# A hybrid decoder layer: the Strassen sums of the second MLP weights made by accumulating DMAs, some signs moved to the other operand, and later squares in FF1

## The chip, the cores and the metric

The kernel runs on one core of one Trainium2 chip. The metric is the device time of one execution in microseconds (us), as the median of several runs. A separate profiled execution gives the trace from which all other times below are read.

## The reference

One decoder layer on x of 1024 x 1024 (tokens x channels, float32), with a conditioning vector c. Cut to what matters:

```python
mod = silu(c) @ w_ada + b_ada
sh1, sc1, gt1, sh2, sc2, gt2 = split(mod, 6)
u = x * (1 + sc1) + sh1
proj = u @ w_in                       # queries, keys, values, DeltaNet inputs, gates
y_a = sliding_window_attention(qa, ka, va, sinks) @ w_oa      # 16 heads, window 128
y_b = gated_deltanet(dq, dk, dv, z, b_raw, a_raw) @ w_ob      # 8 heads of 128, chunks of 64
mixed = (sigmoid(g_a) * y_a + sigmoid(g_b) * y_b) @ w_out
x = layer_norm(ALPHA * x + (1 + gt1) * mixed)
u2 = x * (1 + sc2) + sh2
h = square(relu(u2 @ w_ff1 + b_ff1))                          # 1024 -> 4096: FF1
x = layer_norm(ALPHA * x + (1 + gt2) * (h @ w_ff2 + b_ff2))   # 4096 -> 1024: FF2
```

## The kernel before

Every large float32 product is made of three matmuls: each operand is split in a high part, which ACT rounds to the fast 32-bit type (L215), and a low part, which DVE subtracts (L216); PE adds high x high, high x low and low x high in PSUM. A matmul is 128 x 128 by 128 x 512 nearly everywhere.

The stages, with their place in the profiled execution:

- The adaLN head (to about 60 us): loads of w_ada and x by SP, the modulation rows, and u in its split form.
- The keys stage (about 60 to 260 us; L525 to L697): values and DeltaNet keys of eight heads. A head's projection on PE runs through `fm_unit` (L186 to L188), then come transposes (L664), the decay (L616), a mask on POOL (L627) and key products (L688), with their results stored in DRAM.
- The gate, query and key units and the attention (about 240 to 570 us). `stream_unit` (L236, its matmul is L248) runs 48 matmuls of a 128-channel unit of the projection. In between stand 64 attention slots (L929): the scores on PE (L834 and L835), the maximum and the exponential on DVE and ACT (L842, L849), the joining of the two key blocks' weights on POOL (L853, `join`), the scaling on ACT (L861), a transpose on PE (L877, `att_turn`), its split (L883, L887), a mask on POOL (L894), the product with the values on PE (L909), and for every second slot a store by POOL (L925).
- The head stage (about 580 to 940 us): DeltaNet for eight heads, with the query and value units.
- The two output projections, then the mixing (L1493) with the first layer norm and u2.
- FF1 (about 1240 to 1560 us) and FF2 (to the end), each as one level of the Strassen-Winograd scheme: seven products in place of eight, with sums of blocks formed ahead. FF1 makes 16 block rows x 7 products x 12 matmuls (L1866), FF2 the matmuls of L1926. DVE adds up FF1's blocks (`add_`, L1544), ACT applies relu and square (`square`, L1592; its operations are L1594 and L1595), and `h_sums` (L1613) and `h_sums2` (L1623) form sums of the result for FF2, which go to DRAM (hf_d).

The sums of w_ff2's blocks, which FF2 reads from DRAM (wt_d), are made by POOL. For each of 16 pairs of 128 rows `t_load` (L1681) loads 512 KB twice into SBUF, `t_make` (L1691) makes four differences of 128 x 512 (`sub`, L1436) and stores 512 KB twice in wt_d. Thirteen pairs lie in FF1, three at the start of FF2.

What sets the order: from L702 on, PE, DVE and ACT run in the order in which the code issues their instructions (`tc.manual_schedule(engines=order_all)`). The code keeps a counter of matmuls (`count`) and a heap of events: `at(p, f)` issues f when the counter reaches p, and `after(n, f)` n matmuls later (L197 to L207). SP and POOL are not in that list, and neither is anything ahead of L702: there the tile scheduler orders the instructions itself, by their dependencies and priorities, and an `at` sets for a DMA on SP or POOL no more than where the code issues it. `Q0` (L704) is the counter's value at which the head stage's own plan starts, 48 x the number of units ahead of it; `E0`, `F0` and `G0` are the starts of the mixing, FF1 and FF2.

SP issues nearly all loads, among them those of the projection weights (`load_raw`, L130, tiles wr of 512 KB); an engine's instructions and DMA issues run in order, and one that waits holds up those behind it.

Of the kernel before, what the change touches and what calls it, by code (L numbers as in the profile page):

```python
# [9 lines left out]
F32 = mybir.dt.float32  # L10
# [3 lines left out]
ALU = mybir.AluOpType  # L14
# [3 lines left out]
P = 128  # L18
D = 1024
# [15 lines left out]
def hybrid_layer_kernel(ctx: ExitStack, tc: tile.TileContext,  # L35
                        x, c, w_ada, b_ada, w_in, conv_w, a_log, dt_bias, sinks, dn_norm_w,
                        w_oa, w_ob, w_out, ln1_g, ln1_b, w_ff1, b_ff1, w_ff2, b_ff2,
                        ln2_g, ln2_b, out, dbg=None):
    nc = tc.nc
    x, c, out = x[0], c[0], out[0]  # L40
# [40 lines left out]
    wt_d = dram.tile([D_FF // (2 * P), 2, P, D], F32, name="wt_d")  # L81
# [60 lines left out]
    NPAIR, EARLY = NF // 2, 5  # L142
# [49 lines left out]
    halves = [slice(0, HALF), slice(HALF, 2 * HALF)]  # L192


    events, count, order = [], [0], [0]

    def at(p, f, *args):  # L197
        order[0] += 1
        heapq.heappush(events, (p, order[0], f, args))

    def after(n, f, *args):
        at(count[0] + n, f, *args)
# [275 lines left out]
    for step in ('t0 s0 o00 o01 w0 w1 d4 t1 s1 v203 o10 v235 o11 v256 m0 t2 p2 s2 v304 o20 v346 o21 m1 t3 p3 s3 v404 o30 v446 o31 m2 '  # L478
                 't4 p4 s4 v504 o40 v546 o41 m3 t5 p5 s5 r0 v604 o50 v646 o51 m4 t6 p6 s6 v704 o60 v746 o61 m5 t7 p7 s7 o70 o71 m6').split():
        f, k = step[0], int(step[1])  # L480
# [44 lines left out]
    with tc.tile_pool(name="pa", bufs=2, side="right") as pa:  # L525
        if True:
            ba = pv.tile([P, NT, 16], F32, name="ba")
            for t in range(NT):
                tok = slice(t * P, (t + 1) * P)
                pt = psum("ab"[t % 2], 2) if t < 4 else mm_tile()  # L530
# [12 lines left out]
                if t:  # L543
                    vd = pa.tile([P, 4, 64], F32, tag="vd", name="vd", bufs=1)
                    a, b = (vraw, pv4) if t % 2 == 0 else (pv4, vraw)
# [26 lines left out]
            for m in (13, 11, 9, 7, 5, 3, 1):  # L572
# [5 lines left out]
                                   op0=ALU.mult, op1=ALU.mult)  # L578
# [448 lines left out]
    def ada_part(f, b):  # L1027
# [23 lines left out]
                V.tensor_tensor(out=sc2, in0=g1c, in1=sc2, op=ALU.mult)  # L1051
        after(4, put)

    items = [(f, k) for f in range(KT) for k in range(KT + (f < 4))]
    at(Q0 + 20, ada_open)
    for i, (f, k) in enumerate(items):
# [324 lines left out]
    def mix_done(second, q, t, pt):  # L1381
        r = rs[t]
        rq = r[:, halves[q]]
        tm = pe.tile([P, HALF], F32, tag="t", name="tm", bufs=6)
        V.tensor_tensor(out=tm, in0=pt, in1=gt1[:, halves[q]], op=ALU.mult)
        V.scalar_tensor_tensor(out=rq, in0=rq, scalar=ALPHA, in1=tm, op0=ALU.mult, op1=ALU.add)
        V.bn_stats(out=parts[:, t, q, :], in_=rq)
        if not second:
            return
        st = pe.tile([P, 4], F32, tag="st", name="st", bufs=3)  # L1390
        V.bn_aggr(out=st[:, 0:2], in_=parts[:, t].rearrange("p q s -> p (q s)"))
        lag = {6: 20, 7: 12}.get(t, 1)
        after(lag, lambda: A.activation(out=st[:, 2:3], in_=st[:, 1:2], func=AF.Sqrt, bias=eps_ln))

        def norm():
            V.reciprocal(out=st[:, 3:4], in_=st[:, 2:3])
            V.tensor_scalar(out=r, in0=r, scalar1=st[:, 0:1], scalar2=st[:, 3:4], op0=ALU.subtract, op1=ALU.mult)
            nc.gpsimd.dma_start(out=res_d[t], in_=r)
        after(lag + 3, norm)
# [35 lines left out]
    def sub(E, out, a, b):  # L1435
        E.tensor_tensor(out=out, in0=a, in1=b, op=ALU.subtract)  # L1436
# [49 lines left out]


    w_more()
    for p in [1, 13] + [SEG * s + o for s in (0, 2) for o in (61, 73, 86, 98)] + [3 * SEG + o for o in (79, 85, 106, 114, 128)]:
        at(E0 + p, w_go)  # L1490
        at(E0 + p + 8, w_more)

# [11 lines left out]
    for s in range(4):  # L1504
        q, t0 = (0, 1, 1, 0)[s], 4 * (s // 2)
        if s != 2:
            del wt[:]
        groups = [[0, 1], [2, 3]] if s < 2 else [[4, 5], [6, 7]] if s == 2 else [[4, 5], [6], [7]]
        for ts in groups:
            pts = []  # L1510
            for t in ts:
                tag = ("mm", "a", "mm", "c", "mm", "a")[bank % 6]
                bank += 1
                pts.append(psum(tag, {"mm": 3, "a": 2, "c": 1}[tag]))
            for c in range(4):
                if len(wt) == c:
                    run_events(count[0])
                    wt.append(ready.pop(0))
                for pt, t in zip(pts, ts):
                    mix_mm(pt, slice(t * P, (t + 1) * P), c)  # L1520
            for pt, t in zip(pts, ts):
                at(max(count[0] + (14 if s == 2 and t > 5 else 1), E0 + 28), mix_done, s % 2 == 1, q, t, pt)
                if s % 2 == 1:
                    at(count[0] + 1, u2_done, t, count[0] + {6: 46, 7: 40}.get(t, 34))

# [17 lines left out]
    def add_(E, out, a, b):  # L1543
        E.tensor_tensor(out=out, in0=a, in1=b, op=ALU.add)  # L1544
# [53 lines left out]
    def full(i, c, pt):  # L1598
        t = tls[i, c]
        add_(V, t, t, pt)  # L1600
        after(3, square, i, c)

    def last_block(i, c, pt):
        t = tile_of(i, c)
# [4 lines left out]
    def again(i):  # L1609

        nc.sync.dma_start(out=tile_of(i, 0), in_=hf_d[0, i])

    def h_sums(i):  # L1613

        a11, a21, a22 = tls[i, 0], tls[i, 1], tls[i, 3]
        sa = sums_[i] = big2.tile([P, 2, HALF], F32, tag="h7", name="sa")
        sub(V, sa[:, 1], a11, a21)
        add_(V, a21, a21, a22)
        sub(V, sa[:, 0], a21, a11)
        put(5, i, a21)  # L1620
        nc.sync.dma_start(out=hf_d[5:7, i].rearrange("m p c -> p m c"), in_=sa)

    def h_sums2(i):  # L1623

        sb = big2.tile([P, 2, HALF], F32, tag="l7", name="sb")[:, 0]
        sub(V, sb, tls[i, 2], sums_[i][:, 0])
        put(3, i, sb)


# [40 lines left out]
    for i in range(NPAIR):  # L1670
        e = max(pos[i, 3], pos[i, 7]) + 12
        if i < EARLY:
            at(e - 24, again, i)
        at(e + 12, h_sums, i)
        at(pos[i, 4] + 20, h_sums2, i)

    wpair = {}

    def t_load(n):  # L1681
        if n < T_IN:
            ts = [big2.tile([P, D], F32, tag=f"{c}6", name="wx") for c in "hl"]
        else:
            ts = [wp.tile([P, D], F32, tag="wr", name="wx", bufs=2) for c in "hl"]
        wpair[n] = ts
        for j in range(2):
            f = n + NPAIR * j
            nc.gpsimd.dma_start(out=ts[j], in_=w_ff2[f * P:(f + 1) * P, :])

    def t_make(n):  # L1691
        (b11, b12), (b21, b22) = [[t[:, h] for h in halves] for t in wpair[n]]
        sub(G, b11, b12, b11)
        sub(G, b12, b22, b12)
        sub(G, b22, b22, b11)
        sub(G, b21, b21, b22)
        for j in range(2):
            nc.gpsimd.dma_start(out=wt_d[n, j], in_=wpair[n][j])

    T_IN, T_STEP = 13, 72  # L1700
    for n in range(NPAIR):
        p = pos[EARLY, 1] - 60 + T_STEP * n if n < T_IN else G0 + 60 + T_STEP * (n - T_IN)
        at(p, t_load, n)
        at(p + 24, t_make, n)

# [52 lines left out]
    def rows_sums():  # L1758
        G2, B2 = rows_["G2"], rows_["B2"]
        V.tensor_scalar(out=G2, in0=G2, scalar1=ALPHA, scalar2=None, op0=ALU.mult)  # L1760
        V.tensor_tensor(out=B2, in0=B2, in1=rows_["gt2"], op=ALU.mult)
        V.scalar_tensor_tensor(out=B2, in0=rows_["lb"], scalar=ALPHA, in1=B2, op0=ALU.mult, op1=ALU.add)

    def rr_load(t):
        rr[t] = big.tile([P, D], F32, tag=f"{'hl'[t // 4]}{4 + t % 4}", name="rr")
# [239 lines left out]
```

## Time and profile before

| | |
|---|---|
| median of 3 runs | 1883.41 us (1881.8 to 1889.56) |
| the profiled execution | 1882.44 us |
| its span, first to last instruction | 1880.3 us |
| mean granted TensorE clock | 0.989 of full speed |
| PE busy | 1827.3 us, 97% of the span |
| DVE, ACT, POOL busy | 1309.7, 978.0 and 411.7 us |

Busy time of PE includes matmuls that overlap in its pipeline, so a stretch in which PE is busy all the time may still run at less than its best rate; the granted clock and the number of matmuls of a stretch show that. In a group of instructions the numbers behind the bar are the busy time in us, the mean of one in ns, and the idle time of the engine just before, with what ended it. In a row of a DMA the numbers are KB of one transfer and us from its issue to its landing. Releasers are inferred from semaphore events.

### The profile page before, as it was taken

The numbers are of one execution on the slowest core, as the hardware profiler recorded it, in microseconds if no ns is written. First come the engines' busy times: TensorE is split into PE (matmuls) and PEld (weight loads), VectorE is DVE, ScalarE is ACT, GpSimd is POOL, SyncE is SP. The second block draws the span as 40 slices with busy tenths as digits, with TensorE's granted clock in tenths as the row PEclk, the third lists the DMA queues.
The fourth block names the chain that finished last, engine by engine and source line by source line (L and its number), as shares of the span: only waits on it lengthen the run. The fifth ranks groups of instructions, "written<-read, shape, count | busy, mean of one in ns | idle before, by whom it ended". The sixth has DMA issues, their size and how long they took to land.

```text
span 1880.3 us, 26014 instructions
## 1 busy us (share of the span) xinstructions
PE 1827.3 (97%) x9161; PEld 1509.4 (80%) x9161; DVE 1309.7 (70%) x2409; ACT 978.0 (52%) x2105; POOL 411.7 (22%) x509
## 2 busy tenths in 40 slices
PE   7999999999999999999999999999899999999997
PEld 5977788788888888888878888877687888888886
DVE  7677598998865666666554445788877566676697
ACT  3789666666654454554553322475454555434441
POOL 7323223433331000000001100014545102300000
PEclk7999999999999999999999999999999999999999
DMA  9655632232258454554346543359887549965571
GB/s 258 183 185 194 218 96 82 75 95 70 71 188 224 144 152 129 147 148 133 111 165 213 182 146 135 134 176 312 294 277 267 185 131 405 388 199 169 195 263 45
DMA packets 261644, 337.72 MB, mean 180 GB/s; under 512 B 25237, under 2 KB 170342, under 8 KB 261258
## 3 DMA queue, kind: packets, MB, share of 16 engines
q1 hardware_dynamic: 224042, 215.04, 36.4%
q0 software_dynamic: 30560, 108.44, 16.9%
q10 hardware_dynamic: 6912, 12.59, 1.8%
q8 instruction: 72, 1.18, 0.3%
q14 instruction: 58, 0.48, 0.1%
HBM read 231.40 MB, written 102.51 MB: 178 GB/s over the span
## 4 chain that ended last, share of the span: by engine, by line
PE 75%; DVE 11%; ACT 5%; issue 3%; DMA 2%; POOL 0%; ACTq 0%; SPq 0%; DVEq 0%; POOLq 0%
PE mm L248 33%; PE mm L1926 6%; PE mm L1866 6%; PE b L1926 4%; PE a L1926 4%; PE b L1866 3%; PE mm L1499 2%; DVE wl L216 2%; PE c L1926 2%; PE c L909 2%; PE a L1499 1%; PE a L1866 1%; PE mm L188 1%; PE mm L187 1%; PE mm L186 1%
## 5 line engine op out<-in xcount | busy, mean ns | idle before, releaser
L248 PE MATMUL mm<-uh,wl 128*128 128x512 f32 x800 | 331.3, 414 | 0.0
L248 PE MATMUL mm<-ul,wh 128*128 128x512 f32 x800 | 320.7, 401 | 0.0
L248 PE MATMUL mm<-uh,wh 128*128 128x512 f32 x800 | 317.4, 397 | 0.0
L216 DVE TENSOR_TENSOR sp<-sraw,sp 128x1024 fp32r<-128x1024 f32 x112 | 140.3, 1288 | 70.8 <-ACT sp L215 70.8
L215 ACT ACTIVATE sp<-sraw 128x1024 fp32r<-128x1024 f32 x112 | 112.7, 1054 | 121.6 <-PE b L1926 73.8
L248 PEld LDWEIGHTS mm<-ul,wh 128*128 128x128 f32 x800 | 150.6, 188 | 26.6 <-issue 0.2
L248 PEld LDWEIGHTS mm<-uh,wl 128*128 128x128 f32 x800 | 151.2, 189 | 22.9 <-issue 3.9
L248 PEld LDWEIGHTS mm<-uh,wh 128*128 128x128 f32 x800 | 151.2, 189 | 21.2 <-issue 0.2
L1926 PE MATMUL mm<-sp 128*128 128x512 f32 x528 | 136.5, 390 | 0.5 <-DVE sp L216 0.5
L1436 POOL TENSOR_TENSOR wx<-wx 128x512 f32<-128x512 f32 x64 | 100.3, 1567 | 77.4 <-DMA wx<-in_w_ff_dram 75.7
L1926 PEld LDWEIGHTS mm<-sp 128*128 128x128 f32 x528 | 98.6, 188 | 21.0 <-DVE sp L216 0.9
L216 DVE TENSOR_TENSOR wl<-wr,wh 128x1024 fp32r<-128x1024 f32 x81 | 98.6, 1218 | 8.1 <-ACT wh L215 7.9
L215 ACT ACTIVATE wh<-wr 128x1024 fp32r<-128x1024 f32 x81 | 85.0, 1049 | 22.2 <-PE c L1499 14.0
L216 DVE TENSOR_TENSOR wl<-fraw,wh 128x1024 fp32r<-128x1024 f32 x43 | 61.3, 1426 | 46.1 <-ACT wh L215 46.1
L1926 PE MATMUL a<-sp 128*128 128x512 f32 x336 | 92.5, 389 | 0.0
L1594 ACT ACTIVATE t<-t 128x512 f32<-128x512 f32 x48 | 30.1, 626 | 98.0 <-DVE t L1544 98.0
L1926 PE MATMUL b<-sp 128*128 128x512 f32 (+1 forms) x336 | 80.0, 374 | 0.0
L1169 ACT ACTIVATE vn<-a,brk 128x128 f32<-128x128 f32 x64 | 23.5, 367 | 108.2 <-PE a L1167 107.3
L842 DVE CUSTOM_DVE_ANT_0 nscore<-a,amask,nsink 128x256 f32<-128x256 f32 (+1 forms) x128 | 54.6, 464 | 33.4 <-PE a L835 32.7
L853 POOL TENSOR_TENSOR sm<-sm 128x256 f32<-128x256 f32 x56 | 55.6, 993 | 97.7 <-ACT sm L849 65.0
L1926 PEld LDWEIGHTS a<-sp 128*128 128x128 f32 x336 | 63.1, 188 | 13.1
L1926 PEld LDWEIGHTS b<-sp 128*128 128x128 f32 x336 | 60.5, 188 | 11.2
(520 smaller groups left out, 4718.3 us busy)
## 6 DMA issues: line engine op xcount, KB each, us to landing
wr<-in_w_in_dram SPq DMA_DIRECT2D x60, 512.0 KB, 3.6
sraw<-hf_d SPq DMA_DIRECT2D x56, 512.0 KB, 4.3
fraw<-in_w_ff_dram SPq DMA_DIRECT2D x32, 512.0 KB, 5.1
wx<-in_w_ff_dram POOLq DMA_DIRECT2D x32, 512.0 KB, 6.1
wt_d<-wx POOLq DMA_DIRECT2D x32, 512.0 KB, 4.2
sraw<-wt_d SPq DMA_DIRECT2D x32, 512.0 KB, 4.8
hf_d<-t ACTq DMA_DIRECT2D x48, 256.0 KB, 3.3
sraw<-in_w_ff_dram SPq DMA_DIRECT2D x24, 512.0 KB, 7.0
```

The costliest lines, as they stand in the source:

```text
L215: A.activation(out=hi, in_=src, func=AF.Copy)
L216: after(lag, lambda: V.tensor_tensor(out=lo, in0=src, in1=hi.bitcast(F32), op=ALU.subtract))
L248: T.matmul(ts[half], lhsT=w[:, k, :], rhs=xx[k][:, sl], start=k == 0 and m == 0, stop=k == KT - 1 and m == 2)
L842: V.tensor_tensor_reduce(out=ns[:, i, 1:1 + W], in0=sc[:, i * 2 * P:i * 2 * P + W], in1=amask[:, mo:mo + W], scale=-1.0, scalar=nsink[:, 2 ...
L853: G.tensor_tensor(out=sm[:, :, 1 + P:1 + 2 * P], in0=sm[:, :, 1:1 + P], in1=sm[:, :, 1 + P:1 + 2 * P], op=ALU.add)
L909: T.matmul(av[:, 0:256], lhsT=vt[:, b, :], rhs=p_[:, m, :], start=p_ is full and m == 0, stop=p_ is prods[-1][1] and m == 1)
L1169: after(1, lambda: A.activation(out=vn, in_=Wp[:, 0:P], func=AF.Copy, scale=brk[:, n, h:h + 1]))
L1436: E.tensor_tensor(out=out, in0=a, in1=b, op=ALU.subtract)
L1499: T.matmul(pt, lhsT=m[k][:, tok], rhs=w[:, k % 2, :], start=k == 0 and w is wh and m is mh, stop=k == KT - 1 and m is ml)
L1594: A.activation(out=t, in_=t, func=AF.Relu)
L1866: T.matmul(pt, lhsT=a[:, k0 + k, :], rhs=b[k], start=begin and k == 0 and x_ == 0, stop=k == 3 and x_ == 2, skip_group_check=True)
L1926: T.matmul(to, lhsT=a[:, f, t * P:(t + 1) * P], rhs=b[:, f, lo:up], start=(begin or own) and s % NS == 0 and f == 0 and x_ == 0, stop=s % ...
```

## The change

- The 32 loads, 64 differences and 32 stores of `t_load` and `t_make` go. In their place, in eight batches of two pairs, SP copies two blocks of 1 MB of w_ff2 into wt_d, DRAM to DRAM (`t_copy`), and POOL issues four accumulating DMAs of 512 KB (`t_acc`), which add DRAM rows to DRAM rows: the first two add a half of w_ff2 to a copied half, the third adds the first's result to the other block, and the fourth adds the third's result. They are given counter positions in the head stage (from Q0 + 40 on).
- With additions alone some sums come out with the opposite sign. `h_sums` and `h_sums2` form the other operand with opposite signs (`minus`), and the second half of the row gt2 is negated once (in `rows_sums`).
- `square` of a full FF1 block is issued 14 matmuls after its sum in place of 3, `h_sums` and `h_sums2` 12 matmuls later.
- In the mixing some lags (norm of tile 6, `mix_done` of tile 7, `u2_done`) and four points of its weight splits (`w_go`) move.

```diff
+    def w2_rows(b, n, h):
+        return w_ff2[(b * NPAIR + n) * P:(b * NPAIR + n + TB) * P, h].rearrange("(n p) c -> n p c", p=P)
+
+    def t_copy(n):
+        for b in range(2):
+            nc.sync.dma_start(out=wt_d[n:n + TB, b], in_=w2_rows(b, n, slice(0, D)))
+
+    def t_acc(n, i):
+        one, two = wt_d[n:n + TB, 0], wt_d[n:n + TB, 1]
+        dst, src = [(one[:, :, halves[0]], w2_rows(0, n, halves[1])), (one[:, :, halves[1]], w2_rows(1, n, halves[1])),
+                    (two[:, :, halves[1]], one[:, :, halves[0]]), (two[:, :, halves[0]], two[:, :, halves[1]])][i]
+        nc.gpsimd.dma_start(out=dst, in_=src, accum_op=ALU.add)
+
+    TB = 2
+    for n in range(0, NPAIR, TB):
+        p = Q0 + 40 + 60 * n
+        at(p, t_copy, n)
+        for i in range(4):
+            at(p + (30, 34, 64, 94)[i], t_acc, n, i)
...
-        lag = {6: 20, 7: 12}.get(t, 1)
+        lag = {6: 26, 7: 12}.get(t, 1)
...
-    for p in [1, 13] + [SEG * s + o for s in (0, 2) for o in (61, 73, 86, 98)] + [3 * SEG + o for o in (79, 85, 106, 114, 128)]:
+    for p in [1, 13] + [SEG * s + o for s in (0, 2) for o in (61, 73, 86, 98)] + [3 * SEG + o for o in (79, 100, 112, 118, 130)]:
...
-                at(max(count[0] + (14 if s == 2 and t > 5 else 1), E0 + 28), mix_done, s % 2 == 1, q, t, pt)
+                lag = 14 if s == 2 and t > 5 else 10 if s == 3 and t == 7 else 1
+                at(max(count[0] + lag, E0 + 28), mix_done, s % 2 == 1, q, t, pt)
                 if s % 2 == 1:
-                    at(count[0] + 1, u2_done, t, count[0] + {6: 46, 7: 40}.get(t, 34))
+                    at(count[0] + 1, u2_done, t, count[0] + {4: 30, 5: 36, 6: 48, 7: 42}.get(t, 34) - lag + 1)
...
-        after(3, square, i, c)
+        after(14, square, i, c)
...
+    def minus(out, a, b):
+        V.scalar_tensor_tensor(out=out, in0=a, scalar=-1.0, in1=b, op0=ALU.mult, op1=ALU.subtract)
+
...
-        add_(V, a21, a21, a22)
-        sub(V, sa[:, 0], a21, a11)
+        sub(V, a21, a22, a21)
+        minus(sa[:, 0], a21, a11)
...
-        sub(V, sb, tls[i, 2], sums_[i][:, 0])
+        minus(sb, tls[i, 2], sums_[i][:, 0])
...
-        at(e + 12, h_sums, i)
-        at(pos[i, 4] + 20, h_sums2, i)
-    def t_load(n):
...
-    def t_make(n):
...
+        at(e + 24, h_sums, i)
+        at(pos[i, 4] + 32, h_sums2, i)
...
+        gt = rows_["gt2"][:, halves[1]]
+        V.tensor_scalar(out=gt, in0=gt, scalar1=-1.0, scalar2=None, op0=ALU.mult)
```

More of the change, by code (lines that the diff above doesn't have):

```diff
@@ L1673, in hybrid_layer_kernel @@
             at(e - 24, again, i)
-        at(e + 12, h_sums, i)
-        at(pos[i, 4] + 20, h_sums2, i)
-    wpair = {}
-    def t_load(n):
[L1682 to L1689, printed above, removed]
-    def t_make(n):
[L1692 to L1704, printed above, removed]
+        at(e + 24, h_sums, i)
+        at(pos[i, 4] + 32, h_sums2, i)
     ORDER = (1, 2, 6, 5, 3, 7, 4)
```

## The prediction, made before the changed kernel ran

> **What bounds it now.** I read the page first, then the windows, the waits of PE, the groups of DVE, and the DMA and queue views of the stages that the change enters.
>
> ```profile
> PE 1827.3 (97%) x9161; PEld 1509.4 (80%) x9161; DVE 1309.7 (70%) x2409; ACT 978.0 (52%) x2105; POOL 411.7 (22%) x509
> ```
>
> PE is busy for 97% of the 1880.3 us span (the profiled run took 1882.44 us, the median is 1883.41, so the sum below starts from 1882.4 and needs no correction over 1 us). What can be gained is the little that PE loses; what can be lost is anything that makes PE wait. The windows show both, as busy time of PE, PEld, DVE, ACT and POOL, then PE's granted clock, DMA share and GB/s.
>
> ```profile
> 100.00:140.00 40.00, 39.78 (x211) 30.94 (x210) 33.47 (x93) 35.82 (x89) 12.37 (x20) 1.00 0.53 176
> 140.00:180.00 40.00, 40.00 (x195) 31.17 (x194) 29.65 (x71) 38.49 (x88) 14.88 (x22) 1.00 0.63 213
> ...
> 1260.00:1280.00 20.00, 18.46 (x80) 14.60 (x79) 13.61 (x19) 13.76 (x23) 8.34 (x10) 1.00 0.69 223
> 1280.00:1300.00 20.00, 19.85 (x88) 16.12 (x87) 17.87 (x18) 10.70 (x16) 10.15 (x10) 1.00 0.91 311
> 1300.00:1320.00 20.00, 18.21 (x73) 14.53 (x72) 17.95 (x16) 8.33 (x12) 13.12 (x12) 0.91 0.97 337
> 1320.00:1340.00 20.00, 19.75 (x87) 15.73 (x85) 18.01 (x20) 8.58 (x13) 10.14 (x12) 1.00 0.87 314
> 1340.00:1360.00 20.00, 14.88 (x55) 11.02 (x55) 15.06 (x15) 11.17 (x17) 9.75 (x10) 0.91 0.86 281
> 1360.00:1380.00 20.00, 20.00 (x83) 16.35 (x82) 12.11 (x16) 10.37 (x15) 9.08 (x9) 0.91 0.78 268
> 1380.00:1400.00 20.00, 19.81 (x88) 16.09 (x87) 14.20 (x16) 10.48 (x16) 11.01 (x12) 1.00 0.75 253
> 1400.00:1420.00 20.00, 18.06 (x80) 14.61 (x78) 16.34 (x15) 8.40 (x13) 10.19 (x12) 1.00 0.84 290
> 1420.00:1440.00 20.00, 19.23 (x78) 15.74 (x79) 13.19 (x15) 10.38 (x15) 9.83 (x10) 0.91 0.78 263
> ...
> 1480.00:1500.00 20.00, 20.00 (x90) 16.57 (x89) 12.62 (x16) 11.52 (x17) 0.00 (x0) 1.00 0.43 145
> ...
> 1560.00:1580.00 20.00, 19.54 (x87) 15.86 (x86) 14.22 (x17) 14.28 (x17) 2.10 (x4) 1.00 1.05 407
> ```
>
> In FF1 PE idles while POOL makes the sums (1260 to 1440), and idles no more where POOL is at 0.00. In the keys stage (100 to 180) PE is full, yet ACT is nearly full too.
>
> **FF1: the gain.** Groups of DVE with POOL at work (1270 to 1460), then the same forms without it (1482 to 1540):
>
> ```profile
> L216 DVE TENSOR_TENSOR wl<-fraw,wh 128x1024 fp32r<-128x1024 f32 x27 | 40.2, 1491 | 25.3 <-ACT wh L215 25.3
> L1436 DVE TENSOR_TENSOR sa<-t 128x512 f32<-128x512 f32 x20 | 18.1, 903 | 0.3
> ```
> ```profile
> L216 DVE TENSOR_TENSOR wl<-fraw,wh 128x1024 fp32r<-128x1024 f32 x9 | 11.0, 1225 | 12.6 <-ACT wh L215 12.6
> L1436 DVE TENSOR_TENSOR sa<-t 128x512 f32<-128x512 f32 x6 | 4.2, 692 | 0.1
> ```
>
> DVE's operations are 20 to 30% longer beside POOL's. The change takes all 64 POOL operations, 32 loads and 32 stores out. The ceiling is PE's idle time in the nine windows, 1.54+0.15+1.79+0.25+5.12+0+0.19+1.94+0.77 = 11.8 us, and the clock of 0.91 in four of them, 0.09 x (18.21+14.88+20.00+19.23) = 6.5 us: 18 us. I take **-16** (bounds -8 and -18: the later squares and sums add slack on DVE's and ACT's order, but no row shows each of these lags alone). The Trainium skill, "SBUF — State Buffer", section "Who interferes with whom", says that a DVE instruction with two SBUF inputs and a GpSimd one that reads SBUF exclude each other entirely; the two rows agree (1491 against 1225 ns).
>
> ```profile
> 1220.00:1240.00 20.00, 15.83 (x77) 12.65 (x76) 16.44 (x34) 13.84 (x33) 1.80 (x3) 1.00 0.58 184
> ```
> ```profile
> L803 DVE SCALAR_TENSOR_TENSOR qs<-mm,qs 64x512 fp32r<-64x512 f32 x20 | 13.8, 688 | 0.5
> ```
>
> The signs cost nothing: `minus` does in one scalar_tensor_tensor what one tensor_tensor did, at about its price (688 ns in the q units, on half the partitions, beside 692 ns for sa), and the one new negation of 128x512 in FF2 takes at most that on DVE, which is idle for 5.8 of the 20 us of the last window above. The later lags of the mixing and the moved points of its weight splits work on the passage from the mixing to FF1, where PE loses 4.2 us (1220 to 1240); I give them 0 (bounds -4 and +1).
>
> **Keys stage: the lost cover.** Only PE, DVE and ACT from the solve on are ordered by hand; the keys stage, SP and POOL go by the scheduler, and the change makes it order them anew. On PE at the end of the keys stage, L248 are the first projection units of the hand-ordered part, L688 the last heads' key products. Before:
>
> ```order
> L248 MATMUL mm_2216<-ul0_130,wh_2114 128x512
> L248 MATMUL mm_2216<-uh0_122,wl_2115 128x512
> L248 MATMUL mm_2216<-uh1_123,wh_2114 128x512
> L248 MATMUL mm_2216<-ul1_131,wh_2114 128x512
> L688 MATMUL a_2055<-kT_1861 128x128 x4
> L248 MATMUL mm_2216<-uh1_123,wl_2115 128x512
> L248 MATMUL mm_2216<-uh2_124,wh_2114 128x512
> ```
> And after:
> ```order
> L688 MATMUL a_1981<-kT_1720 128x128 x4
> L688 MATMUL a_1990<-kT_1720 128x128 x4
> L664 MATMUL b_2027<-ident_89,kT_1861 128x128 x4
> L664 MATMUL c_2036<-ident_89,kT_1861 128x128 x4
> L616 MATMUL a_2005<-gT_1098,sel_1094 128x512
> L616 MATMUL a_2014<-gT_1098,sel_1094 128x512
> L688 MATMUL a_2055<-kT_1861 128x128 x4
> L688 MATMUL a_2064<-kT_1861 128x128 x4
> L248 MATMUL mm_2097<-uh0_122,wh_1723 128x512
> ```
>
> 106 L248 matmuls stood ahead of the last L688; now none does. The heads' ACT and DVE work is as long as before, so PE waits through it bare.
>
> ```profile
> 1365.87 5.44 PE mm L1866 x24
> ```
>
> At this chain's 5.44/24 = 0.227 us for a matmul of the same form, that is 106 x 0.227 = **+24** (bounds 0, if ACT and DVE finish as much earlier, and +50, if their interleaving gets worse too).
>
> **The sums by DMA.** Sixteen SP copies of 1 MB and 32 POOL accumulates of 512 KB, eight batches of four. Within a batch the third accumulate waits for the first, the fourth for the third; POOL stands at that wait with everything behind it. The diff names the head stage, but SP and POOL are not ordered by hand, and the scheduler has put the batches earlier. On POOL in attention before (L853 joins two halves of a slot's weights, and PE's L877 turn needs it; L894 masks):
>
> ```order
> L853 TENSOR_TENSOR sm_2606<-sm_2606 128x2x128
> L894 AFFINE_SELECT pl_2591<-ph_2590 128x512
> L925 DMA attn_d_69<-at_2574 128x256
> L894 AFFINE_SELECT pl_2647<-ph_2646 128x512
> L853 TENSOR_TENSOR sm_2661<-sm_2661 128x2x128
> ```
> And after (in_w_ff2 as source: first and second; wt_d as source: third and fourth):
> ```order
> L1067 DMA wt_d_86<-in_w_ff2_dram 2x128x512
> L853 TENSOR_TENSOR sm_2606<-sm_2606 128x2x128
> L894 AFFINE_SELECT pl_2647<-ph_2646 128x512
> L1067 DMA wt_d_86<-in_w_ff2_dram 2x128x512
> L853 TENSOR_TENSOR sm_2661<-sm_2661 128x2x128
> L925 DMA attn_d_69<-at_2684 128x256
> L894 AFFINE_SELECT pl_2705<-ph_2704 128x512
> L1067 DMA wt_d_86<-wt_d_86 2x128x512
> L853 TENSOR_TENSOR sm_2719<-sm_2719 128x2x128
> L894 AFFINE_SELECT pl_2759<-ph_2758 128x512
> L1067 DMA wt_d_86<-wt_d_86 2x128x512
> ```
>
> Six batches stand so, one in the keys stage, one just ahead of the first join. The pace of the slots and POOL's slack (a join's idle time before it, last bracket):
>
> ```profile
> L925 POOL DMA_DIRECT2D attn_d<-at x32: 542/557/953, 263.2 to 566.9; - x32
> ```
> ```profile
> 336.34 1.67 POOL L853 TENSOR_TENSOR sm<-sm 128x256 f32<-128x256 f32 x1 [3.39 <-issue]
> ```
>
> Two slots take (566.9-263.2)/31 = 9.8 us, one 4.9. The slack is 3.4. With D from an accumulate's issue to its landing, a batch costs PE (D-9.8-3.4) + (D-4.9-3.4), each if positive. No row shows an accumulate; the nearest, with KB and us to landing:
>
> ```profile
> wr<-in_w_in_dram SPq DMA_DIRECT2D x60, 512.0 KB, 3.6
> wx<-in_w_ff_dram POOLq DMA_DIRECT2D x32, 512.0 KB, 6.1
> wt_d<-wx POOLq DMA_DIRECT2D x32, 512.0 KB, 4.2
> ```
> ```profile
> khh<-khh POOLq DMA_DIRECT2D x8, 128.0 KB, 7.2
> ```
>
> By the rows of 512 KB and 128 partitions D is 4.2 to 6.1 and nothing waits. But the new patterns have an outer size of 2 (the order shows 2x128x512 and 2x8x16384). If only two engines carry them, the best rate of a window, 407 GB/s over 16 engines, is 25.4 each: 524 KB / 50.8 GB/s = 10.3 us, and twice, 20.6, if the destination's reading counts too. The khh row, 7.2 us for a quarter of the bytes, is nearer to that end than to 4.2, so I take 20.6: (7.4+12.3) x 6 = **+118** (bounds 0 and, with two accumulates sharing engines, +200). The two batches ahead of attention have no slots under their waits: up to 2 x 2 x 20.6 = 82, less POOL's idle share; **+35** (bounds 0 and +82). The Trainium skill, "DMA: Bandwidth & Descriptors", section "Why a DMA increments its semaphore by 16 and not by 1", states that an engine count is the largest up to 16 that divides the slowest dimension; by it both patterns get 2 engines, and it speaks against this change. No view here shows a count of engines.
>
> SP's copies pass weight loads (L130). After, where the gates begin:
>
> ```order
> L1061 DMA wt_d_86<-in_w_ff2_dram 2x8x16384
> L130 DMA wr_2296<-in_w_in_dram 128x8x128
> L130 DMA wr_2387<-in_w_in_dram 128x8x128
> L813 DMA ga_d_72<-gate_2295 128x1024
> L1061 DMA wt_d_86<-in_w_ff2_dram 2x8x16384
> L130 DMA wr_2521<-in_w_in_dram 128x8x128
> ```
> ```profile
> 54.85 0.32 SPq L457 DMA_DIRECT2D rows<-in_b_ff_dram  x1
> ...
> 227.34 11.25 SPq L130 DMA_DIRECT2D wr<-in_w_in_dram  x2
> ...
> 335.56 31.16 SPq L130 DMA_DIRECT2D wr<-in_w_in_dram  x3
> ```
>
> Eleven copies of 1 MB in some 140 us (227.34 to 366.72) need 11 x 20.6 = 227 us on two engines, 87 more than there is; much of it lies under the same waits of POOL, so **+25** (bounds 0 and +87).
>
> **Sum**: 1882.4 - 16 + 24 + 118 + 35 + 25 = 2068.4, say **2068 us**. The case's own range: with 10.3 us, 2.0 x 6 = 12 for attention and 8 for the rest, 1882.4-16+24+20 = 1910; at the high bounds of waits, 1882.4-16+24+200+82+25 = 2197.
>
> **Rivals.** (1) *The patterns spread on all engines* and D is 4 to 6: no wait in attention, only the lost cover and 6+6 us in the keys stage, where the first batch stands bare: 1882.4-16+24+12 = 1902. For it: all 512 KB rows; against: the outer size of 2. (2) *Faster*: the transfers hide and ACT and DVE, free of 106 interleaved matmuls' order, end the keys stage earlier by what PE lost. Then only FF1 counts: 1882.4-16 = 1866. It decides when the lost cover is under 7 us; ACT at 38.49 of 40 speaks against. With 12 us of lost cover it ends at no change, 1878. (3) *Traffic*: every batch is bound by its engines, copies and accumulates share two: (16.8+16.8) MB / 50.8 GB/s = 661 us, from 55 (the row of L457, behind which the first copy stands) to 716, while the last batch stands behind some 28 joins, near 263 + 28 x 4.9 = 400 us: 1882.4-16+316 = 2182.
>
> **Chances.** Two engines with waits 0.56, traffic 0.10, spread 0.23, no change 0.04, faster 0.07. Half a per cent, 9 us, is about what a measurement of this kernel can tell from no change. So faster 0.07, same 0.05 (a cheap end of the spread case with it), slower 0.88. Range 1892 to 2190: the spread case at its middle, and the traffic case.
>
> **What would show it.** Right: PE's idle rows in attention, L877 waiting for ACT or POOL's L853 late by 10 us and more, POOL idle until DMA wt_d, accumulates over 15 us to landing, no PE idle in FF1 between 1260 and 1440 of before's time, and PE idle at L664, L616 and L688. Wrong: accumulates landing in 4 to 8 us, or a keys stage as dense as before's.

## The result, and the profile after

The changed kernel takes 2261.52 us (median of 4 runs, 2260.63 to 2268.28) beside 1883.06 us before: a ratio of 1.2009, 95% interval 1.1973 to 1.2045. The forecast of 2068 us had the sign, but less than half of the size (185 of 378 us), and the range (to 2190 us) missed it.

The page of the profiled execution (span 2259.3 us): PE's busy time grew by 54 us although it issues the same 9161 matmuls, and its share fell to 83%. The last row is the granted clock in 40 slices of 56 us, in tenths; before it was at 9 in all slices but the first.

```profile
PE 1881.7 (83%) x9161; PEld 1549.1 (69%) x9161; DVE 1269.1 (56%) x2410; ACT 971.1 (43%) x2102; POOL 330.6 (15%) x413
...
PEclk8978787776777799999999999999999999999999
```

Where the time went is read from the first and last start of a few lines. In a line's view of the kernel before, the two numbers ahead of the semicolon are these starts (L688 key products, L853 joins, L1866 FF1, L1926 FF2):

```profile
L688 PE MATMUL a<-kT x128: 270/275/275, 111.8 to 216.9; 128*128 128x128 f32 x128
...
L853 POOL TENSOR_TENSOR sm<-sm x56: 726/742/2264, 244.5 to 552.6; 128x256 f32<-128x256 f32 x56
...
L1866 PE MATMUL mm<-mh,wh x112: 387/389/628, 1268.2 to 1563.3; 128*128 128x512 f32 x112
...
L1926 PE MATMUL b<-sp x336: 279/389/390, 1609.6 to 1870.0; 128*128 128x512 f32 x144, 128*128 128x256 f32 x24
```

The same lines after (FF1 is now L1865, FF2 L1925; L925 is the attention's store, 263.2 to 566.9 before):

```profile
L688 PE MATMUL a<-kT x128: 270/276/553, 173.0 to 278.6; 128*128 128x128 f32 x128
...
L853 POOL TENSOR_TENSOR sm<-sm x56: 728/1020/2807, 358.1 to 939.3; 128x256 f32<-128x256 f32 x56
...
L925 POOL DMA_DIRECT2D attn_d<-at x32: 542/568/1462, 428.7 to 953.6; - x32
...
L1865 PE MATMUL mm<-mh,wh x112: 389/389/390, 1658.9 to 1936.5; 128*128 128x512 f32 x112
...
L1925 PE MATMUL b<-sp x336: 279/389/390, 1988.6 to 2249.0; 128*128 128x512 f32 x144, 128*128 128x256 f32 x24
```

| stretch | before | after | difference |
|---|---|---|---|
| start to first key product | 111.8 | 173.0 | +61.2 |
| first to last key product | 105.1 | 105.6 | +0.5 |
| last key product to first join | 27.6 | 79.5 | +51.9 |
| first join to last attention store | 322.4 | 595.5 | +273.1 |
| that store to FF1 | 701.3 | 705.3 | +4.0 |
| FF1, first to last mm product | 295.1 | 277.6 | -17.5 |
| from there to FF2's last b product | 306.7 | 312.5 | +5.8 |

The sum is +379.0, the difference of the spans. What POOL and PE wait for over the whole span (us in all, times, longest):

```profile
POOL wt_d L1067 <- DMA wt_d<-wt_d: 171.6, 8, 27.7
POOL wt_d L1067 <- DMA wt_d<-in_w_ff_dram: 132.8, 6, 33.5
```
```profile
PE b L877 <- ACT sm L861: 228.4, 14, 32.2
PE c L909 <- DVE at L922: 26.3, 11, 9.5
```

POOL stands 304 us at the third and fourth accumulates, 235 us of it in attention (358 to 954 us) and 69 us ahead of the first join, and PE waits 228 us at the slot's transpose. POOL's timeline shows one such case: 33.48 us idle ahead of the third accumulate, with the join (L853) right behind it, then 23.38 us ahead of the fourth:

```profile
365.68 1.08 POOL L894 TENSOR_SCALAR_AFFINE_SELECT pl<-ph 128x512 fp32r<-128x512 f32 x1 [1.18 <-DVE ph L887]
400.24 1.91 POOL L1067 DMA_DIRECT2D wt_d<-wt_d  x1 [33.48 <-DMA wt_d<-in_w_ff_dram]
401.38 1.54 POOL L853 TENSOR_TENSOR sm<-sm 128x256 f32<-128x256 f32 x1
402.06 1.44 POOL L894 TENSOR_SCALAR_AFFINE_SELECT pl<-ph 128x512 fp32r<-128x512 f32 x1
426.88 1.94 POOL L1067 DMA_DIRECT2D wt_d<-wt_d  x1 [23.38 <-DMA wt_d<-wt_d]
```

The DMA view gives the landing (KB, then the median in us): an accumulate takes 26 to 36 us, where the prediction took 20.6.

```profile
wt_d<-in_w_ff_dram POOLq DMA_DIRECT2D x16, 512.0 KB, 36.0
wt_d<-wt_d POOLq DMA_DIRECT2D x16, 512.0 KB, 26.3
```

The wait has a second price. The window of the disturbed attention after, and then attention before (PE's busy time and count, ..., granted clock, DMA share, GB/s):

```profile
360.00:800.00 440.00, 196.18 (x850) 159.83 (x850) 143.46 (x344) 111.85 (x322) 103.06 (x107) 0.71 0.38 84
```
```profile
263.00:567.00 304.00, 297.34 (x1569) 248.41 (x1569) 253.47 (x627) 196.59 (x564) 117.10 (x152) 1.00 0.30 98
```

At before's pace 850 matmuls keep PE busy for 297.34 x 850/1569 = 161 us, an estimate that takes the same mix of matmuls in both windows. After they take 196, at a granted clock of 0.71: of 440 us some 244 are idle and, by this estimate, 35 are slower running.

Ahead of the first join the chain of waits shows the other cost, weight loads that took 3.6 us in the median before (start, then us):

```profile
105.03 28.61 DMA wr<-in_w_in_dram
...
286.27 33.11 DMA wr<-in_w_in_dram
```

### The profile page after: what moved, and what is told of

The parts are those of the page before. It is cut to its first block, busy times and chain, and to the rows that moved or that the text cites. A ratio compares the mean times of both kernels' runs of the same rounds, so it can differ in the third digit from the quotient of the medians.

```text
span 2259.3 us, 25888 instructions
## 1 busy us (share of the span) xinstructions
PE 1881.7 (83%) x9161; PEld 1549.1 (69%) x9161; DVE 1269.1 (56%) x2410; ACT 971.1 (43%) x2102; POOL 330.6 (15%) x413
## 2 busy tenths in 40 slices
DMA packets 318764, 338.17 MB, mean 150 GB/s; under 512 B 82101, under 2 KB 227206, under 8 KB 318122
## 4 chain that ended last, share of the span: by engine, by line
PE 57%; issue 13%; DMA 12%; DVE 9%; ACT 5%; POOL 2%; SPq 1%; ACTq 0%; POOLq 0%; DVEq 0%
PE mm L248 23%; PE mm L1925 5%; DMA wt_d<-wt_d 3%; PE mm L1865 3%; PE a L1925 3%; PE b L1925 3%; DMA wt_d<-in_w_ff_dram 3%; DMA wr<-in_w_in_dram 3%; PE b L1865 3%; PE mm L1521 2%; PE c L1925 1%; PE a L1865 1%; PE a L1521 1%; DVE wl L216 1%; DMA attn_d<-at 1%
## 5 line engine op out<-in xcount | busy, mean ns | idle before, releaser
L248 PE MATMUL mm<-uh,wl 128*128 128x512 f32 x800 | 339.4, 424 | 2.6 <-DVE wl L126 2.6
L248 PE MATMUL mm<-uh,wh 128*128 128x512 f32 x800 | 326.4, 408 | 13.1 <-ACT gate L811 13.1
L248 PE MATMUL mm<-ul,wh 128*128 128x512 f32 x800 | 329.1, 411 | 0.0
L877 PE MATMUL b<-ident,sm 128*128 128x128 f32 x128 | 29.6, 313 | 228.4 <-ACT sm L861 228.4
L877 PEld LDWEIGHTS b<-ident,sm 128*128 128x128 f32 x128 | 19.0, 148 | 242.5 <-ACT sm L861 234.5
L216 DVE TENSOR_TENSOR sp<-sraw,sp 128x1024 fp32r<-128x1024 f32 x112 | 132.8, 1220 | 83.7 <-ACT sp L215 83.6
L861 ACT ACTIVATE sm<-sm,stat 128x128 f32<-128x128 f32 x128 | 44.2, 394 | 271.7 <-POOL sm L853 264.0
L1925 PE MATMUL mm<-sp 128*128 128x512 f32 x528 | 138.4, 394 | 3.1 <-DVE sp L216 1.9
L856 DVE RECIPROCAL stat<-stat 128x2 f32<-128x2 f32 x64 | 10.2, 160 | 192.9 <-ACT sm L849 192.5
L1925 PEld LDWEIGHTS mm<-sp 128*128 128x128 f32 x528 | 99.8, 190 | 24.4 <-DVE sp L216 2.2
L1925 PE MATMUL a<-sp 128*128 128x512 f32 x336 | 93.2, 392 | 0.0
L1067 POOL DMA_DIRECT2D wt_d<-wt_d x16 | 31.0, 1936 | 340.2 <-DMA wt_d<-wt_d 171.6
L1925 PE MATMUL b<-sp 128*128 128x512 f32 (+1 forms) x336 | 80.0, 374 | 0.0
L216 DVE TENSOR_TENSOR wl<-fraw,wh 128x1024 fp32r<-128x1024 f32 x43 | 52.6, 1223 | 40.0 <-ACT wh L215 40.0
L1925 PEld LDWEIGHTS a<-sp 128*128 128x128 f32 x336 | 63.5, 189 | 13.3
```

The source lines that it names most:

```text
L216: after(lag, lambda: V.tensor_tensor(out=lo, in0=src, in1=hi.bitcast(F32), op=ALU.subtract))
L248: T.matmul(ts[half], lhsT=w[:, k, :], rhs=xx[k][:, sl], start=k == 0 and m == 0, stop=k == KT - 1 and m == 2)
L856: V.reciprocal(out=st[:, 4:6], in_=st[:, 2:4])
L861: A.activation(out=o, in_=o, func=AF.Copy, scale=st[:, 4 + i:5 + i])
L877: T.transpose(tp[:, i * P:(i + 1) * P], sm[:, i, 1 + (nb - 1) * P:1 + nb * P], ident)
L1067: nc.gpsimd.dma_start(out=dst, in_=src, accum_op=ALU.add)
```

## The experiments

The theory to be tested: an outer size of 2 puts a transfer on few engines, so it lands late, and what stands behind it on POOL, SP and those engines waits. The rivals: an accumulate is slow in itself; the place alone is wrong; the moved positions, not POOL's absence, make FF1 faster. Ratios are to the kernel before on the same chip, with 95% intervals.

**e1, both patterns spread.**
```diff
-            nc.sync.dma_start(out=wt_d[n:n + TB, b], in_=w2_rows(b, n, slice(0, D)))
+            nc.sync.dma_start(out=wt_d[n:n + TB, b].rearrange("n p c -> p n c"),
+                              in_=w2_rows(b, n, slice(0, D)).rearrange("n p c -> p n c"))
...
-        nc.gpsimd.dma_start(out=dst, in_=src, accum_op=ALU.add)
+        nc.gpsimd.dma_start(out=dst.rearrange("n p c -> p n c"), in_=src.rearrange("n p c -> p n c"), accum_op=ALU.add)
```


> The same 16 copies and 32 accumulates of the same sizes, with the 128 rows as the outer size (128x2x1024 and 128x2x512) in place of 2. Theory (an outer size of 2 puts a transfer on few engines, and that makes an accumulate land after 26 us and more): landing 5 to 10 us, weight loads wr back under 8 us, 104 projection matmuls again ahead of the last key product, time 1862 to 1885. Rival (an accumulate from DRAM to DRAM is slow by itself, reading two operands): landing still over 18 us, POOL waits of 10 us and more remain, time over 1950.

Measured 1946.86 us, 1.0326 (1.0306 to 1.0346). Its DMA view:

```profile
wt_d<-in_w_ff_dram SPq DMA_DIRECT2D x16, 1024.0 KB, 22.9
...
wt_d<-in_w_ff_dram POOLq DMA_DIRECT2D x16, 512.0 KB, 11.9
wt_d<-wt_d POOLq DMA_DIRECT2D x16, 512.0 KB, 8.5
```

With the pattern (and the other places that the scheduler then gave the transfers; e6 and e8 below keep the place) 315 of 378 us went; attention is as before (317.4 to 640.8 from the first join to the last store, 323.4 us). But the time missed the expectation by 60 us. The first join comes 73 us late (317.4 after 244.5): nearly all batches now stand ahead of it (the last accumulate is issued at 328.1 us), and a copy of 1 MB takes 22.9 us there even when spread.

**e2, only the copies spread**, and **e3, only the accumulates spread** (one of the two edits above each).

> Only the copies get 128 as the outer size; the accumulates keep 2 and their places between the attention's joins. Theory (few engines for each accumulate is enough for the waits): landing 15 to 25 us without the copies' traffic beside it, POOL waits for wt_d of 100 to 250 us, PE waits at L877, weight loads fast, the projection matmuls (109) again ahead of the last key product; time 1980 to 2100. Rival (the copies' occupation of the shared engines is what makes accumulates slow): landing under 12 us, waits mostly gone, time 1870 to 1910.

> Only the accumulates get 128 as the outer size; the copies keep 2, and no projection matmul stands ahead of the last key product, as in the changed kernel. Theory: accumulates land within 10 us once their copy is there, but an accumulate and the weight loads still wait for the slow copies, so wr loads of 20 to 30 us remain and the keys stage still ends 40 to 100 us late; time 1920 to 2060. Rival (the waits come from the accumulates alone): keys stage late by the lost cover of 24 us only, time 1890 to 1910.

Measured 2143.60 us, 1.1359 (1.1335 to 1.1384), and 2084.53 us, 1.1052 (1.1033 to 1.1070). With the copies spread the accumulates still land after 27.5 us (the first two) and 27.0 us (the others), so the rival falls: the copies lengthen the first two, which took 36.0 us in the changed kernel, and not the others (26.3). The time is above the 2100 expected. With the accumulates spread they land after 9.5 and 7.4 us in the median, but up to 29.4 us, and POOL still stands 108 us (31.1 + 76.9) at them over the whole run; that kernel too is 25 us above its expected range. Attention (first join to last store) takes 479.8 and 415.6 us.

**e4, no accumulates, copies spread**: `t_acc` is not issued.

> The copies with 128 as the outer size, no accumulates at all: the sums of the second MLP weights are left out, FF2 works on the bare blocks, with all its loads and matmuls. It shows what the change without its accumulates is worth. Theory (POOL's sums in SBUF cost FF1 16 us, copies of this form cost nothing): 1862 to 1870, FF1 under 300 us from its first mm product to its last. Rival (the gain lies under other work, or the copies cost as much): 1878 to 1890.

Measured 1883.60 us, 0.9987 (0.9975 to 0.9999). FF1 is shorter by 17.5 us, as expected:

```profile
L1866 PE MATMUL mm<-mh,wh x112: 389/389/389, 1290.7 to 1568.3; 128*128 128x512 f32 x112
```

but the first join is 16 us late (260.5), and the stretches with the moved positions take the rest (706.6 beside 701.3 us from the last attention store to FF1, 311.4 beside 306.7 in FF2). These stretches are of a profile 8 us above the median. The rival holds for the total.

**e11, no accumulates, copies as in the change.**

> The changed kernel without any accumulate (the sums are left out); the copies keep the outer size of 2. No projection matmul stands ahead of the last key product, as in the changed kernel. Theory (copies on few engines hold up the weight loads that use the same engines): wr loads of 10 to 30 us where before had 3.6, keys stage 40 to 90 us late, attention within 30 us of before; 1915 to 1990. Rival (the copies do no harm by themselves, only the order does): keys stage late by the lost cover of about 24 us, 1890 to 1905.

Measured 1988.38 us, 1.0537 (1.0516 to 1.0558), the upper end of the theory's range. The chain of waits shows the copies' harm by themselves:

```profile
275.99 29.49 DMA wr<-in_w_in_dram
307.91 21.70 DMA wr<-in_w_in_dram
```

The packet records of this trace show how the copies do it. Of the 1024 packets of 512 bytes of the load issued at 275.99 us, 896 (14 parts of 16) have started by 283 us. Then no packet of 512 bytes starts until 298.8 us: the copy's packets of 64 KB, 2.4 us each, run two at a time until 299.4 us, and the load's other 128 packets come behind them. Attention takes 348.3 us beside 322.4 with these copies and no accumulate.

From the last key product to the first join this kernel takes 61.1 us (260.4 to 321.5); e4, with spread copies and the projection matmuls back ahead, 29.8 (230.7 to 260.5). The 31 us between them hold the lost cover (24 by the forecast) and these loads; the two are not separated by any run.

**e10, the first two accumulates of each batch alone**: `for i in range(2)`, so none waits for another.

> The changed kernel without the third and fourth accumulate of each batch (two of four sums are left out): copies and the first two accumulates stay with the outer size of 2, and no accumulate waits for another. Theory (attention lost its 273 us to POOL standing at the third and fourth): first join to last attention store 322 to 350 us, PE's wait at L877 under 20 us, the keys stage still 60 to 110 us late; 1940 to 1990. Rival (the traffic on few engines slows attention whatever POOL does): that stretch over 420 us, total over 2050.

Measured 2100.23 us, 1.1140 (1.1100 to 1.1181): the theory, as put, falls, and the rival's two numbers hold. POOL waits 3.5 us for wt_d in all, yet attention takes 436.6 us (353.7 to 790.3). DVE's waits in it name another path:

```profile
DVE at L922 <- DMA attn_d<-at: 95.8, 7, 44.3
```

A store of 128 KB that landed in 2.2 us in the median and 5.2 at most before takes up to 57.3 us when it is issued behind accumulates, DVE may not reuse its tile, and PE waits at the values' product (97.6 us). So POOL's standing is not the only way by which attention loses; stores that land late behind the accumulates are the second. Copies alone do not bring it about: in e11 the same wait of DVE's is 0.2 us. Whether the store waits for the accumulate's engines or for its place in POOL's DMA queue, which both use, no run separates. In the changed kernel this wait of DVE's is 42.1 us in all.

**e12, batches of four pairs**: `TB = 4`.

> The changed kernel with batches of four pairs: 8 copies of 2 MB and 16 accumulates of 1 MB, whose outer size is 4 in place of 2. If the number of engines is that size, each engine moves as much as before and an accumulate lands in 24 to 36 us, as in the changed kernel, with half as many waits: 2000 to 2150. If the landing goes by the bytes (an accumulate is slow by itself), it takes 50 us and more, and the time stays at 2200 or over.

Measured 2104.42 us, 1.1154 (1.1133 to 1.1175).

```profile
wt_d<-in_w_ff_dram POOLq DMA_DIRECT2D x8, 1024.0 KB, 42.2
wt_d<-wt_d POOLq DMA_DIRECT2D x8, 1024.0 KB, 26.8
```

Twice the bytes with twice the outer size land in the same time (26.8 beside 26.3 us; the first two, which meet the copies, took 42.2 beside 36.0). The packet records of the traces show why. The changed kernel's accumulate issued at 400.24 us is 256 packets of 2 KB, 177 ns each in the median, and they run two at a time for most of the 23 us from 402.95 to 425.99. In e12 (the one issued at 498.33 us) 512 such packets run four at a time, again for 23 us. With 128 as the outer size (e7 below, the one issued at 701.22 us) 256 packets of 178 ns run sixteen and more at a time for most of the 4 us that they take. A packet takes as long in all three; what differs is how many run at once, and that goes with the outer size. There is one more difference: an outer size of 2 adds 57,344 packets of 8 bytes (the pages count 82,101 packets under 512 bytes, and 24,757 in e3), some 8 ns each. In the lone transfer they end within 6 us of its issue, while the 2 KB packets run on for 20 us, so they are not what makes it long. Over the whole landing an accumulate moves 262 KB / 26.3 us = 10 GB/s on each of two engines.

**e5, the moved positions alone**, in the kernel before.
```diff
-        after(3, square, i, c)
+        after(14, square, i, c)
```
with the change's other lags and points.

> The kernel before, with only the change's moved positions: later squares and sums in FF1, the mixing's lags and weight splits. No DMA, no sign. Theory (these positions are what makes the passage to FF1 3.7 us and FF2 5.8 us longer in the changed kernel, since FF1's last sums then stand on DVE ahead of FF2's first split): passage and FF2 longer by 3 to 10 us in all, FF1 with POOL's sums shorter by 0 to 5; time 1884 to 1893 beside 1883. Rival (they help, and FF2 pays for the transfers): FF1 shorter by 3 us and more, FF2 as before; 1875 to 1882.

Measured 1896.71 us, 1.0044 (1.0024 to 1.0063), 8 us slower by the ratio and above both ranges. FF1 stays at 296.2 us beside 295.1, so the later squares do not shorten it under POOL's sums. The passage, here from the last matmul group of the output projection ya (1050.1 us before) to FF1, is 221.5 us beside 218.1, and FF2 by the table's ends 311.5 beside 306.7.

**e6, held to the head stage, spread**: each batch ahead of its copies gets a DMA from the head's stored output, which orders it truly.
```diff
+    def t_batch(n):
+        for b in range(2):
+            nc.sync.dma_start(out=wt_d[n, b][0:1, 0:P], in_=og_d[n // TB][0:1, 0:P])
+        t_copy(n)
...
                 nc.gpsimd.dma_start(out=og_d[h], in_=d["sz"])
+                t_batch(TB * h)
```


> The changed kernel with 128 rows as the outer size of copies and accumulates, and each batch held back to the head stage by a true dependency: a 512-byte DMA from the head's stored output in DRAM into the block that the copy then overwrites. The keys stage and attention then stand in the order of before (106 projection matmuls ahead of the last key product). Theory (place and pattern make the loss): keys stage and attention as before, FF1 -17, passage +4, FF2 +6: 1872 to 1882. Rival (the transfers cost their time wherever they stand): head stage longer by 20 us and more, over 1895.

The same **with the old positions, e7**:

> As the run before, and the moved positions of squares, sums, lags and weight splits put back to those of the kernel before. Theory (the positions cost the passage and FF2 9 us and FF1 needs them little): 1863 to 1872, faster than both kernels. Rival (FF1's gain of 17 us comes from the later squares and not from POOL's absence): FF1 shorter by under 8 us, time 1875 to 1885.

and **with the change's patterns and positions, e8**:

> The changed kernel with its own patterns (outer size 2), each batch held back to the head stage as in the two runs before, positions as changed. It tells place from pattern. Theory (the waits cost because attention's joins stand behind them on POOL; in the head stage POOL has slack, and only loads on the shared engines suffer): landing again 20 to 30 us, time 1880 to 1960. Rival (with such slow transfers any stage stalls as attention did): over 2050.

Measured 1891.37 us, 1.0023 (1.0006 to 1.0040); 1884.08 us, 0.9987 (0.9970 to 1.0005); and 2333.66 us, 1.2355 (1.2319 to 1.2391), slower than the change itself. The first two keep the earlier stages as before (first join 249.6 and 247.3) and FF1's gain, the second without any late square:

```profile
L1867 PE MATMUL mm<-mh,wh x112: 389/389/389, 1291.1 to 1568.5; 128*128 128x512 f32 x112
```

277.4 us: the gain is POOL's absence. They give it back where the heads' batches run: in e7 the output projection ya takes 110.8 us beside 100.7, the stretch from the last attention store to it 390.4 beside 382.5, and both theories' times are missed. Whether the transfers' traffic or POOL's waits take it is not separated. The third settles the rival of the place: e6 and e8 differ in the pattern alone, 1891 and 2334 us. With an outer size of 2 POOL stands 318 us at its accumulates there too, the head stage, whose recurrence stands behind POOL's loads, stalls as attention did, and the theory's 1880 to 1960 falls. PE's waits between 570 and 1480 us:

```profile
PE mm L248 <- DVE ga L1312: 108.8, 3, 41.2
PE a L1190 <- DVE rhs L1182: 88.3, 11, 26.8
PE a L1180 <- DVE St L1205: 64.6, 5, 30.0
```

**e9, held to FF1**, spread, old positions, where POOL has no other work. SP's copies and holding DMAs first:

> 128 rows as the outer size, the moved positions put back, and each batch held back to FF1 by a 512-byte DMA from one of FF1's stored blocks: POOL then has no other work there, and the stages ahead stand as in the kernel before. Theory (a wait on POOL costs only what is queued behind it, and FF1's gain comes from POOL no longer reading SBUF beside DVE): keys stage to mixing as before, FF1 shorter by 14 to 18 us, FF2 as before: 1862 to 1872, faster than both. Rival (the DRAM traffic in FF1 delays the loads of its weights and FF2's first operands): FF1 gains under 8 us or FF2 loses as much, 1875 to 1890.

Measured 1912.72 us, 1.0135 (1.0111 to 1.0159). FF1 takes 323.3 us: SP's queue stands 51.8 us at its holding DMAs with the stores of FF1's sums behind it, DVE waits 24.8 us for such stores, and PE waits for ACT (21.6 + 7.3 us). Then **e13, the same by POOL alone** (`nc.gpsimd` in place of `nc.sync`):

> As e9, but POOL issues the copies and the small holding DMAs too, so that SP's queue is as in the kernel before and nothing but POOL's own queue waits for them. Theory (in e9 FF1 grew because SP's stores of FF1's sums stood behind a holding DMA or a copy): FF1 from its first mm product to its last 275 to 285 us, all other stages as before; 1862 to 1872, faster than both kernels. Rival (the traffic itself holds up FF1's stores and loads): FF1 over 295 us, total 1880 or more.

Measured 1893.14 us, 1.0042 (1.0028 to 1.0056). FF1 has its gain (1273.7 to 1551.3, 277.6 us) with the issuing queue alone changed, so SP's queue was the cause; but FF2 is 23 us longer:

```profile
DVE G L1762 <- DMA G<-in_ln_g_dram: 19.8, 1, 19.8
```

POOL loads the rows of the second norm behind the last batch, from 1580 us on, and before from 1545. Three runs tried to mend it: all batches released by the mixing's last block (e14), all by one early block of FF1 (e15), and, spaced as in e13, only the last batch put behind these rows (`HOLD` ends in 15 in place of 11).

> As e13, but all batches are released by the mixing's last stored block, some 20 us ahead of FF1 in place of well inside it, and the batches overlap on POOL's queue. In e13 FF1 was 17 us shorter and FF2 23 us longer: DVE waited there for the row G of the second layer norm, which POOL loads behind the last batch. Theory (only that queue place was wrong): FF1 275 to 285 us, FF2 305 to 309 us, all else as before; 1864 to 1874, faster than both kernels. Rival (the traffic of the transfers beside FF2's first loads is the cause): FF2 still over 315 us, 1880 or more.

> As e13, but all eight batches are released together by the same stored block of FF1 as the first one there (some 1310 us), so that the batches overlap on POOL's queue as in e14 and end earlier, without e14's traffic on FF1's first blocks. Theory (FF2's 23 us of e13 were POOL's queue place alone, e14's 33 us in FF1 were loads of its first blocks, which DVE awaits): FF1 276 to 286 us, the rows of the second norm issued by 1550 us, FF2 305 to 312 us; 1866 to 1877, faster than both. Rival (in FF1 too the denser transfers hold up its loads and stores): FF1 over 295 us, 1882 or more.

> As e13, with its spacing of one batch after another, but the last batch released by FF1's last stored block, so that POOL issues the rows of the second layer norm ahead of it. Theory (spaced transfers leave FF1 its gain, 278 us as in e13, and FF2's 23 us were the rows' place in POOL's queue): FF1 275 to 284 us, rows issued by 1560 us, FF2 305 to 312 us; 1866 to 1876, faster than both. Rival (as in e15, one stage gives back what the other gains, whatever the queue order): 1880 or more.

Measured 1895.94 us, 1.0048 (1.0029 to 1.0067); 1883.82 us, 0.9999 (0.9979 to 1.0018); and 1877.55 us, 0.9958 (0.9945 to 0.9972). In all three FF2 is as before (306 us), so its 23 us were the queue place. FF1 of e14 is 327 us in a profile slower than its median: its first blocks are loaded back soon after their store, and DVE waits for that:

```profile
DVE sa L1463 <- DMA t<-hf_d: 44.6, 5, 11.6
```

Denser transfers (e15) cost FF1 what it gained (293.8 us); spaced ones leave some of it. The last is faster than the kernel before by 0.4%, 7 us, just outside its expected range; its profile, the slowest of its five runs, has FF1 at 290.0 us, and why it is 277.6 in one and 290.0 in the other at the same spacing stays open.

## Why the prediction was wrong in its size, step by step

- **FF1, -16**: -17.5, right, and by the reason given: with POOL out, the split of fraw takes DVE 1223 ns where it took 1491,

```profile
L216 DVE TENSOR_TENSOR wl<-fraw,wh 128x1024 fp32r<-128x1024 f32 x41 | 50.2, 1223 | 38.0 <-ACT wh L215 38.0
```

and e7 shows it without the later squares.
- **Moved positions, 0 (bounds -4 and +1)**: wrong. +4.0 from the last attention store to FF1, 3.7 of it in the passage behind ya, and +5.8 in FF2, past the upper bound; e5 shows 3.4 and 4.8 from the positions alone, e7 without them 1.1 and 1.3. At the start of FF2 three late sums of FF1, 0.7 us each, stand on DVE ahead of a split that PE awaits (1948.5 to 1950.6 us); the rest of the 5.8 us is not traced.
- **Keys stage, +24, +35 and +25, together 84**: 61.2 + 0.5 + 51.9 = 113.6. The kinds were right (lost cover, POOL's first waits, late weight loads). The key products themselves took no longer (105.6 beside 105.1 us); the projection matmuls that ran among them before come behind them. e11, without any accumulate, has its first join 77.0 us late (321.5 beside 244.5), where +24 and +25 allowed 49; if the two add up, the accumulates' share is then some 37 us, near the +35. So the step that came out short is "much of it lies under the same waits of POOL, so +25": loads of 28.6 and 33.1 us stood in the chain themselves, before any slot had started.
- **Attention, "so I take 20.6: (7.4+12.3) x 6 = +118"**: the step that failed; +273.1, which is 155 of the 193 us between the forecast's +186 and the span's +379. The place and the mechanism were right: POOL stands at the third and fourth accumulate with the join behind. What was mis-sized is D first of all: 36.0 us for the first two and 26.3 for the others. The prediction's own formula then gives (36.0-13.2) + (26.3-8.3) = 40.8 us a batch, 245 us for six, as an estimate. Of D the packets alone are 23 us, close to the 20.6; some 3 us from the issue to the first packet were put at nothing, and so was the traffic of the copies beside the first two (36.0 us, 27.5 with spread copies in e2). The sum had two further costs at nothing. PE's granted clock was 0.71 in that stretch, some 35 us by the estimate above. And the attention's own stores land late behind the accumulates, a path that needs no wait of POOL's: e10 loses 114 us in attention without them (436.6 beside 322.4), 26 of which the copies alone also cost (e11). These costs overlap, so they do not add up to the rest one by one.
- **The chain and the traffic as alternatives**: the traffic rival (2182 us) was the nearest number, but that does not bear it out. It was given a chance of 0.10 as a case that replaces the waits; the runs show both at once.
- **The engines**: the sentence on the Trainium skill, "DMA: Bandwidth & Descriptors", section "Why a DMA increments its semaphore by 16 and not by 1", holds as far as the runs go: with outer sizes of 2, 4 and 128 the packets run two, four and sixteen and more at a time, 2 and 4 give the same landing for the same bytes of an engine (26.3 and 26.8 us), and 128 gives 8.5 us in e1.
- **Spread transfers as harmless (1902 us)**: e1 took 1946.86. A landing of 8.5 to 11.9 us for 512 KB is about twice that of the 512 KB rows (4.2 to 6.1 us), and copies of 1 MB took 22.9 us among them.

## What to carry to other kernels

Before a DMA is moved, read its outer size and what stands behind it in the queue that issues it: where the queue waits in order for a landing, as POOL's did here, everything behind waits too. A transfer that is off SBUF and off the compute engines is not off the path. Look in the order of the built program for where a scheduler has put it, and hold it by a true dependency if the place matters. In this case PE's waits cost more than their length, with a granted clock of 0.71 among them, and stores issued behind long transfers kept their tiles for up to 57 us.

## What the runs showed of the hardware

- A DRAM-to-DRAM accumulate with an outer size of 2 ran two packets at a time, with 4 four, with 128 sixteen and more; a packet of 2 KB took 177 ns each time. Over the landing that is about 10 GB/s on each of two or four engines (512 KB in 26.3 us, 1 MB in 26.8).
- With 128 as the outer size the packets of 512 KB were through in 4 us in place of 23, but the landing fell only from 26.2 to 6.7 us (the two transfers whose packets are told under e12): some 3 us of both lie ahead of the first packet and behind the last.
- A load that is spread over the engines lands with its slowest share: beside a copy with outer size 2, 14 of 16 parts of a 512 KB weight load had started within 7 us of its issue, and the rest came behind the copy's packets of 64 KB, some 23 us after it (e11: 29.49 us in the chain, beside 3.6 us in the median before).
- In a stretch where PE was idle for more than half of the time the mean granted clock was 0.71; in the same stage before it was 1.00.
